# A two-layer encoder on one Trainium2 core: the first projection by k tile, products ahead of the data, earlier bias tables, a shorter sub-norm

## The chip, the cores and the metric

One core of a Trainium2 chip runs the whole kernel as one program. The metric is the device time of an execution in microseconds (us); lower is better. Engines are named as in the profile: PE is the matrix engine (PEld its weight loads), DVE the vector engine, ACT the scalar engine, POOL the GpSimd engine, SP the engine that issues nearly all DMAs here.

## What is computed

The input x is 512 tokens by 1024 channels in float32. Two layers follow one another, and each is a mixer with a residual sum and then an MLP with a residual sum:

- RMS norm, then layer 0's mixer: dilated sliding-window attention, 16 heads of 64 channels in three groups (6, 5 and 5 heads), with a bias from a 32 x 16 table, looked up by relative position, added to the logits; the groups' outputs are weighted by a softmax over their log-sum-exp.
- Layer 1's mixer: differential attention, 8 heads, two softmaxes per head, `a = p0 - lambda * p1` with lambda computed from a 4 x 64 input, `o = a @ v`, an RMS norm of o over its 128 channels (the sub-norm), then the output projection.
- Each MLP: `relu(x @ w_in)^2 @ w_out` with 4096 hidden channels.
- A last RMS norm.

The result has to agree with a float32 reference.

## The kernel before

**Layout and products.** Activations are kept transposed, eight tiles of 128 channels by 512 tokens (`hT[d]`). Every large float32 product is made of three products of rounded operands (`mm3`, L168 to L171): weights high by activations high, weights low times activations high, and the remaining cross term, each a 128x128 by 128x512 matmul. So each operand is split into a high part (an ACT copy, `whi`, `Ah`) and a low part (a DVE subtraction, `wlo`, `Al`). Weights come in units of 1 MB, 1024 rows by 256 columns for a projection. `fetch` (L140) reads a unit into `raw` and splits it in two halves by columns (L158 ACT, L159 DVE); `raw`, `whi` and `wlo` have two buffers each. `linear_steps` (L173) runs a unit: for each of its two tiles of 128 output columns eight k tiles of three products into one PSUM bank. There are eight banks: two `acc`, three `s`, two `t`, one `o`.

**The start.** L317 fetches the first unit (queries 0 to 255) in four pieces, with the reads of x between them. `Norm.feed` (L228) makes `Ah` on ACT and `Al` on DVE for each k tile and gathers the sum of squares, with POOL doing some squares and all sums (L236 to L243). L428 and L429 run the first queries and the first keys, column tile by column tile, into banks from `wide`; the results are held until the norm's factor is known (`rstd`, `rows`, then `release`), because the projection runs on the unnormalised x. `tables()` (L357) then looks up the bias tables: it reads the 33 x 2048 one-hot matrix, rounds it on ACT, makes eight 33-row products into `s` banks, copies them out on DVE (L375) and writes them to DRAM as `fd` (L376). `hankel` (L419) reads the biases of each query row back from `fd`, in rows that overlap: `B0` (six heads, 256 wide) and two parts of `B1` (L435 to L438).

**Layer 0's attention.** `probs0(p)` (L462) takes a pair of heads: logits on PE (L345, L346) into `s` banks, bias and row minimum in one DVE operation (L451), the exponential on ACT (L453), transposes on PE (L485) and a DVE copy (L487). The order in the program is probs0(0), probs0(1), qk0(1) (queries and keys of pair 2 and 3), values0(0), probs0(2), and so on (L569 to L592).

**Layer 1's attention.** `attend1` (L762) goes through 8 heads by 4 blocks of 128 queries: logits, softmaxes, `cf`, the combination on DVE (L785), transposes (L791), the product with v (L800) into one `o` bank for the four blocks of a head, the sub-norm of the block (`subnorm`, L802 to L812: a Square on ACT with its row sum, then five small POOL operations), after the fourth block one DVE product (`on`, L845) and the transposes back (`turn`, L814, L817). The head's `o` bank is free for the next head only when `on` has read it. `wo1_first` (L870) is the half of the output projection that needs heads 0 to 3 only, eight column tiles of 12 products each; `wo1_last` (L874) is the other half, five of whose column tiles are placed behind marked instructions by `tc.issue_after`.

**What sets the order.** A planner reorders the instructions by a simulated timeline: an instruction that comes later in the program may be placed ahead on its engine if its operands are ready and nothing earlier is. On the chip every engine then runs its own list strictly in that order. `tc.issue_after(x)` forbids the planner to put the block's PE instructions ahead of x. SP issues the DMAs in order, and a DMA that waits holds up those behind it.

Of the kernel before, what the change touches and what calls it, by code (L numbers as in the profile page):

```python
# [19 lines left out]
P = 128  # L20
# [7 lines left out]
MASKED = 1.0e30  # L28

# [52 lines left out]
def tile_encoder(ctx: ExitStack, tc: tile.TileContext, x, rel_bias, gains, norm_final_g,  # L82
# [18 lines left out]
    def s_tile():  # L101
        return ps_s.tile([P, 512], F32, tag="s", name="s_ps")
# [22 lines left out]

    hT = [hpool.tile([P, SEQ], F32, tag=f"h{d}", name=f"h{d}") for d in range(KT)]
# [13 lines left out]
    def fetch(between=None):  # L140
# [4 lines left out]
        src = w[r0:r0 + kt * P, c0:c0 + ncol].rearrange("(k p) c -> p k c", p=P)  # L145
# [8 lines left out]
        for i, (k, c) in enumerate(pieces):  # L154
            if between:
                nc.sync.dma_start(raw[:, k, c], src[:, k, c])
                between(i)
            nc.scalar.copy(hi[:, k, c], raw[:, k, c])  # L158
            nc.vector.tensor_sub(lo[:, k, c], raw[:, k, c], f32(hi[:, k, c]))  # L159
        ready.append((hi, lo))  # L160
# [59 lines left out]
    class Norm:  # L220
# [7 lines left out]
        def feed(self, d, start=False):  # L228
# [5 lines left out]
            if start:  # L234
                if d == 0:
                    nc.gpsimd.tensor_mul(self.acc, hT[d], hT[d])  # L236
                    return
                sq = spool.tile([P, SEQ], F32, tag="nsq", name="nsq")
                if d < 4:
                    nc.gpsimd.tensor_mul(sq, hT[d], hT[d])  # L240
                else:
                    nc.scalar.activation(sq, hT[d], AF.Square)
                nc.gpsimd.tensor_add(self.acc, self.acc, sq)  # L243
            elif d == 0:
                nc.scalar.activation(self.acc, hT[d], AF.Square)
            else:
                sq = spool.tile([P, SEQ], F32, tag="nsq", name="nsq")
                nc.scalar.activation(sq, hT[d], AF.Square)  # L248
                eng = nc.vector if d == KT - 1 else nc.gpsimd
# [61 lines left out]
    def load_x(*ds):  # L311
        for d in ds:
            nc.sync.dma_start(hT[d], x[d * P:(d + 1) * P, :])
# [29 lines left out]
    def logits(S, q, k, m, qs, ks):  # L343

        nc.tensor.matmul(S, q[m][:, qs], k[m][:, ks], start=True, stop=False)  # L345
        nc.tensor.matmul(S, q[2 + m][:, qs], k[m][:, ks], start=False, stop=True)  # L346
# [10 lines left out]
    def tables():  # L357
        tab = stp.tile([33, 16], F32, name="tab")
        nc.vector.memset(tab[32:33, :], MASKED)
        nc.sync.dma_start(tab[0:32, :], rel_bias)  # L360
        oh = stp.tile([33, E_END], F32, name="oh")
        nc.sync.dma_start(oh, onehot)
        ohr = stp.tile([33, E_END], F32R, name="ohr")
        nc.scalar.copy(ohr, oh)
        th = stp.tile([33, 16], F32R, name="th")
        tl = stp.tile([33, 16], F32R, name="tl")
        nc.vector.tensor_copy(th, tab)
        nc.vector.tensor_sub(tl, tab, f32(th))
        fsb = stp.tile([16, E_END], F32, name="fsb")
        for c in range(E_END // 512):  # L370
            s = slice(c * 512, (c + 1) * 512)
            ps = s_tile()
            nc.tensor.matmul(ps[0:16, :], th, ohr[:, s], start=True, stop=False)
            nc.tensor.matmul(ps[0:16, :], tl, ohr[:, s], start=False, stop=True)
            nc.vector.tensor_copy(fsb[:, s], ps[0:16, :])  # L375
        nc.sync.dma_start(fd, fsb)  # L376

        lam4 = stp.tile([P, 4, 64], F32, name="lam4")
        nc.sync.dma_start(lam4.rearrange("p a b -> p (a b)"),
                          b_lambda.rearrange("a b -> (a b)").unsqueeze(0).broadcast_to([P, 256]))  # L380
        lprod = stp.tile([P, 2, 64], F32, name="lprod")
        lsum = stp.tile([P, 2], F32, name="lsum")
# [24 lines left out]
    held = []  # L407

    def release():
        for f, ct, ps in held:  # L410
            f(ct, ps)

# [22 lines left out]
    hankel(B0, 0, 6, E_G0 + 64, 256)  # L435
    B1 = l0p.tile([P, 10, P], F32, name="B1", bufs=1)
    hankel(B1[:, 0:5, :], 6, 5, E_G1, P)
    hankel(B1[:, 5:10, :], 11, 5, E_G2, P)  # L438
# [130 lines left out]
    probs0(0)  # L569
    probs0(1)  # L570
    qk0(1)
    values0(0)
    probs0(2)
# [188 lines left out]
    def attend1(fill):  # L762
# [39 lines left out]
        def subnorm(b, r0, O, rs4):  # L802
# [144 lines left out]
```

## Time and profile before

| what | value |
|---|---|
| time, median of 3 runs | 1233.21 us (1232.64 to 1233.25) |
| profiled execution, its own time | 1232.82 us |
| profiled execution, span from first to last instruction | 1231.0 us |
| PE busy | 1206.0 us, 98% of the span, 6096 matmuls |
| DVE, ACT, POOL busy | 637.5, 499.3, 116.3 us |
| granted PE clock, mean | 0.993 |

The span is what the trace covers; the device time is 1.8 us longer. A PE row of the profile names the line, the output and input tiles and the shapes; "xN" is how many instructions were merged. The matmuls overlap in the trace, so the time from one start to the next is what counts, not the length shown. A float32 product that isn't split appears as two entries. Times in brackets are idle time of that engine before the instruction and what ended it.

### The profile page before, as it was taken

Reading aid. Unit: us, or ns where it says so; the run is one execution under the profiler, and the core shown is the slowest. Engines: PE = TensorE matmul, PEld = TensorE weight load, DVE = VectorE, ACT = ScalarE, POOL = GpSimd, SP = SyncE. Lnnn points to the kernel's source line nnn. Section 1 sums busy time; section 2 is a strip of 40 time slices with the busy share of each in tenths; the row PEclk is TensorE's granted clock in tenths of the full one; section 3 lists DMA queues with packets and bytes.
Section 4 is the critical chain, followed back from the end, with each engine's and each line's share of the span. In section 5 each row is a group of like instructions: output and inputs, shape, how many; then the busy total and the mean of one; then the engine's idle time right before and its main releaser. Section 6 shows DMA issues by size and latency. Waiting matters only on the chain.

```text
span 1231.0 us, 15250 instructions
## 1 busy us (share of the span) xinstructions
PE 1206.0 (98%) x6096; PEld 1020.2 (83%) x6096; DVE 637.5 (52%) x1039; ACT 499.3 (41%) x905; POOL 116.3 (9%) x219
## 2 busy tenths in 40 slices
PE   7989999999999999999999999998999999999997
PEld 5778878888888888888888998986888888888897
DVE  7764455645433434434478677673754334344333
ACT  5452433434322323313357667653544223133133
POOL 5000000210000000000201232322300000000012
PEclk9989999999999999999999999998999999999999
DMA  7261222233223333223422333121333223332211
GB/s 226 72 123 56 69 69 69 69 103 103 87 86 102 103 103 102 82 90 103 147 81 87 99 124 104 65 85 52 103 103 102 78 95 103 103 103 99 80 62 69
DMA packets 108307, 115.73 MB, mean 94 GB/s; under 512 B 4507, under 2 KB 101915, under 8 KB 108187
## 3 DMA queue, kind: packets, MB, share of 16 engines
q1 hardware_dynamic: 108236, 114.75, 30.0%
q8 instruction: 48, 0.79, 0.3%
q14 instruction: 23, 0.19, 0.0%
HBM read 112.50 MB, written 2.24 MB: 93 GB/s over the span
## 4 chain that ended last, share of the span: by engine, by line
PE 94%; DVE 2%; DMA 2%; ACT 1%; POOL 0%; issue 0%; SPq 0%; POOLq 0%; DVEq 0%; ACTq 0%
PE acc L169 15%; PE acc L171 15%; PE acc L170 15%; PE s_ps L170 13%; PE s_ps L171 13%; PE s_ps L169 13%; PE o_ps L800 2%; PE s_ps L345 1%; PE s_ps L346 1%; PE t_ps L791 1%; DMA B<-fd 1%; PE o_ps L525 1%; PE s_ps L494 1%; PE o_ps L529 1%; PE t_ps L485 0%; DMA h<-in_x_dram 0%
## 5 line engine op out<-in xcount | busy, mean ns | idle before, releaser
L158 ACT CAST whi<-raw 128x1024 fp32r<-128x1024 f32 (+1 forms) x194 | 192.7, 1039 | 392.8 <-PE s_ps L170 217.1
L159 DVE TENSOR_TENSOR wlo<-raw,whi 128x1024 fp32r<-128x1024 f32 (+1 forms) x194 | 233.7, 1241 | 22.9 <-ACT whi L158 22.5
L171 PE MATMUL acc<-Ah,wlo 128*128 128x512 f32 x472 | 185.9, 394 | 0.0
L169 PE MATMUL acc<-Ah,whi 128*128 128x512 f32 x472 | 185.8, 394 | 0.0
L170 PE MATMUL acc<-Al,whi 128*128 128x512 f32 x472 | 185.7, 393 | 0.0
L169 PE MATMUL s_ps<-Ah,whi 128*128 128x512 f32 x360 | 141.6, 394 | 5.7 <-ACT whi L158 5.5
L170 PE MATMUL s_ps<-Al,whi 128*128 128x512 f32 x360 | 142.1, 395 | 1.8 <-DVE Al L233 1.7
L171 PE MATMUL s_ps<-Ah,wlo 128*128 128x512 f32 x360 | 141.3, 393 | 0.0
L169 PEld LDWEIGHTS acc<-Ah,whi 128*128 128x128 f32 x472 | 89.0, 189 | 18.6 <-ACT sp L338 0.5
L171 PEld LDWEIGHTS acc<-Ah,wlo 128*128 128x128 f32 x472 | 88.8, 188 | 18.7 <-DVE wlo L159 0.5
L170 PEld LDWEIGHTS acc<-Al,whi 128*128 128x128 f32 x472 | 88.9, 188 | 18.1 <-issue 0.5
L169 PEld LDWEIGHTS s_ps<-Ah,whi 128*128 128x128 f32 x360 | 68.2, 190 | 20.3 <-ACT whi L158 5.5
L170 PEld LDWEIGHTS s_ps<-Al,whi 128*128 128x128 f32 x360 | 68.1, 189 | 17.6 <-DVE Al L233 3.8
L171 PEld LDWEIGHTS s_ps<-Ah,wlo 128*128 128x128 f32 x360 | 68.3, 190 | 14.2 <-DVE wlo L159 0.3
L644 ACT ACTIVATE u<-u 128x512 f32<-128x512 f32 x64 | 40.0, 628 | 96.6 <-DVE u L643 95.9
L250 POOL TENSOR_TENSOR nacc<-nacc,nsq 128x512 f32<-128x512 f32 x18 | 27.5, 1529 | 527.1 <-ACT nsq L248 526.6
L653 DVE TENSOR_TENSOR h<-h,s_ps 128x512 f32<-128x512 f32 x33 | 22.7, 688 | 105.4 <-PE s_ps L171 105.4
L643 DVE SCALAR_TENSOR_TENSOR u<-s_ps,rB 128x512 f32<-128x512 f32 x40 | 27.6, 691 | 83.8 <-PE s_ps L171 77.1
L775 DVE CUSTOM_DVE_ANT_0 p<-s_ps,bias 128x512 f32<-128x512 f32 x64 | 43.4, 688 | 31.0 <-PE s_ps L346 20.8
L171 PE MATMUL s_ps<-Bh,wlo 128*128 128x512 f32 x152 | 59.2, 389 | 0.0
L169 PE MATMUL s_ps<-Bh,whi 128*128 128x512 f32 x152 | 59.2, 389 | 0.0
L170 PE MATMUL s_ps<-Bl,whi 128*128 128x512 f32 x152 | 59.1, 389 | 0.0
(237 smaller groups left out, 2269.0 us busy)
## 6 DMA issues: line engine op xcount, KB each, us to landing
raw<-in_mlp_w_in_dram SPq DMA_DIRECT2D x32, 1024.0 KB, 5.3
raw<-in_mlp_w_out_dram SPq DMA_DIRECT2D x32, 1024.0 KB, 5.2
raw<-in_b_w_qkv_dram SPq DMA_DIRECT2D x12, 1024.0 KB, 5.2
raw<-in_a_w_qkv_dram SPq DMA_DIRECT2D x11, 1024.0 KB, 5.2
bias<-fd SPq DMA_DIRECT2D x16, 448.0 KB, 3.6
raw<-in_a_w_o_dram SPq DMA_DIRECT2D x4, 1024.0 KB, 5.2
raw<-in_b_w_o_dram SPq DMA_DIRECT2D x4, 1024.0 KB, 5.2
h<-in_x_dram SPq DMA_DIRECT2D x8, 256.0 KB, 5.1
```

Of the source, the lines that this page charges most:

```text
L158: nc.scalar.copy(hi[:, k, c], raw[:, k, c])
L159: nc.vector.tensor_sub(lo[:, k, c], raw[:, k, c], f32(hi[:, k, c]))
L169: nc.tensor.matmul(ps, ahi, bhi, start=first, stop=False)
L170: nc.tensor.matmul(ps, ahi, blo, start=False, stop=False)
L171: nc.tensor.matmul(ps, alo, bhi, start=False, stop=last)
L250: eng.tensor_add(self.acc, self.acc, sq)
L345: nc.tensor.matmul(S, q[m][:, qs], k[m][:, ks], start=True, stop=False)
L643: nc.vector.scalar_tensor_tensor(u, ps, 0.0, nm.rB, op0=ALU.max, op1=ALU.mult)
L644: nc.scalar.activation(u, u, AF.Square)
L653: nc.vector.tensor_add(hT[ct], hT[ct], ps)
L775: nc.vector.tensor_tensor_reduce(out=xt, in0=S, in1=bias[h][m][:, b * P:b * P + SEQ], scale=1.0, scalar=3.0e38, op0=ALU.add, op1=ALU.min, ...
L800: marks["PV"] = nc.tensor.matmul(O[:, b, :], aT[:, k, :], v[:, k, es], start=k == 0, stop=k == NB - 1)
```

## The change

- **First units by k tile.** `fetch` loses its special form. The first two units (first queries, first keys) are read in slices of one k tile: for each d, x's tile (256 KB) and 128 KB of each unit, 24 reads in all. `split_first(d)` makes the operands of k tile d; then four banks (three `s`, one `acc`) each get three products of that k tile. All squares are now made by ACT, and POOL only adds (the last sum is DVE's).
- **Idle products.** `WARM` = 14 float32 products of the identity with itself stand ahead of everything on PE, into a `t` bank.
- **Tables.** The one-hot matrix is read by a DMA that POOL issues, straight into the rounded type. The four parts of the table are made after k tiles 2 to 5, in `t` banks, and copied out by ACT. `B0` is read next; the two `B1` reads come after the second unit of keys; lambda's operations come after values0(0).
- **Second queries.** `rstd` and `rows` get a high priority. The second unit of queries follows at once, into the `o` bank and an `acc` bank, and is held; the four first banks are released after its first product. Its two tiles are taken out after probs0(0) and probs0(1), and the second unit of keys runs after that.
- **Sub-norm.** The factor is folded: `es = EPS * s0^2` is made early on POOL, the Square carries 1/128, and behind it stand two POOL operations, a sum and a power.
- **Output projection.** Of `wo1_first`, the third and fourth column tile of the second unit may not stand ahead of the last logits of head 7's block 2 and block 3.

```diff
+WARM = 14
...
+    idle = t_tile()
+    for i in range(WARM):
+        nc.tensor.matmul(idle[:, 0:P], ident, ident, start=True, stop=True)
...
-        parts = 2 if w is b_w_qkv or w is b_w_o else 2
-        pieces = [(slice(0, kt), slice(c * ncol // parts, (c + 1) * ncol // parts)) for c in range(parts)]
-        if between:
-            pieces = [(slice(k, k + 4), c) for _, c in pieces for k in (0, 4)]
-        else:
-            nc.sync.dma_start(raw, src)
...
+        nc.sync.dma_start(raw, w[r0:r0 + kt * P, c0:c0 + ncol].rearrange("(k p) c -> p k c", p=P))
+        for i in range(2):
+            c = slice(i * ncol // 2, (i + 1) * ncol // 2)
+            nc.scalar.copy(hi[:, :, c], raw[:, :, c])
+            nc.vector.tensor_sub(lo[:, :, c], raw[:, :, c], f32(hi[:, :, c]))
...
-    load_x(0)
-    fetch(lambda i: load_x(*((1, 2), (3, 4), (5,), (6, 7))[i]))
-    for d in range(KT):
-        norm.feed(d, True)
...
+    def load_first(d):
+        nc.sync.dma_start(hT[d], x[d * P:(d + 1) * P, :])
+        for src, raw, hi, lo in first:
+            nc.sync.dma_start(raw[:, d, :], src[:, d, :])
+
+    def split_first(d):
         norm.feed(d, True)
+        for src, raw, hi, lo in first:
+            nc.scalar.copy(hi[:, d, :], raw[:, d, :])
+            nc.vector.tensor_sub(lo[:, d, :], raw[:, d, :], f32(hi[:, d, :]))
+        norm.square(d, True)
...
+    def load_tables():
+        nc.vector.memset(tab[32:33, :], MASKED)
+        nc.sync.dma_start(tab[0:32, :], rel_bias)
+        nc.gpsimd.dma_start(ohr, onehot)
+
+    def table(c):
+        if c == 0:
+            nc.vector.tensor_copy(th, tab)
+            nc.vector.tensor_sub(tl, tab, f32(th))
+        s = slice(c * 512, (c + 1) * 512)
+        ps = t_tile()
+        nc.tensor.matmul(ps[0:16, :], th, ohr[:, s], start=True, stop=False)
+        nc.tensor.matmul(ps[0:16, :], tl, ohr[:, s], start=False, stop=True)
+        nc.scalar.copy(fsb[:, s], ps[0:16, :])
+        if c == 3:
+            nc.sync.dma_start(fd, fsb)
...
-    run(linear_steps(0, KT, 256, norm.xs, out_q0, bank=wide, hold=held))
-    run(linear_steps(0, KT, 256, norm.xs, out_k0, bank=wide, hooks=[(4, norm.rstd), (8, lambda: norm.rows(-0.125)), (12, release)]))
-    tables()
+    load_first(0)
+    load_first(1)
+    load_tables()
+    for d in range(2, KT):
+        load_first(d)
+    banks = [s_tile(), s_tile(), s_tile(), acc_tile()]
+    for d in range(KT):
+        split_first(d)
+        for i, ps in enumerate(banks):
+            _, _, hi, lo = first[i // 2]
+            s = slice((i % 2) * P, (i % 2 + 1) * P)
+            mm3(ps, hi[:, d, s], lo[:, d, s], norm.xs[0][d], norm.xs[1][d], d == 0, d == KT - 1)
+        if 2 <= d < 6:
+            table(d - 2)
...
     hankel(B0, 0, 6, E_G0 + 64, 256)
+    held = []
+    with tc.high_priority():
+        norm.rstd()
+        norm.rows(-0.125)
+
+    def release():
+        for i, ps in enumerate(banks):
+            (out_q0, out_k0)[i // 2](i % 2, ps)
+
+    spare_banks = [acc_tile, o_tile]
+    run(linear_steps(2, KT, 256, norm.xs, out_q0, bank=lambda: spare_banks.pop()(),
+                     hooks=[(1, release)], hold=held))
...
     probs0(0)
+    for f, ct, ps in held[:1]:
+        f(ct, ps)
     probs0(1)
-    qk0(1)
+    for f, ct, ps in held[1:]:
+        f(ct, ps)
+    run(linear_steps(2, KT, 256, norm.xs, out_k0))
+    hankel(B1[:, 0:5, :], 6, 5, E_G1, P)
+    hankel(B1[:, 5:10, :], 11, 5, E_G2, P)
     values0(0)
+    lam()
...
+            es = l1p.tile([P, 1], F32, tag="es", name="es", bufs=4)
+            nc.gpsimd.tensor_scalar(es, st[:, b, 2:3], st[:, b, 2:3], EPS, op0=ALU.mult, op1=ALU.mult)
+            return pr[0], es
...
-            nc.scalar.activation(sq, O[:, b, :], AF.Square, accum_out=ss)
-            rs = rs4[:, b, :]
-            nc.gpsimd.tensor_mul(rs, ss, r0)
-            nc.gpsimd.tensor_mul(rs, rs, r0)
-            nc.gpsimd.tensor_scalar(rs, rs, 1.0 / P, EPS, op0=ALU.mult, op1=ALU.add)
-            nc.gpsimd.tensor_tensor(rs, rs, mhalf[:, 0:1], op=ALU.pow)
-            nc.gpsimd.tensor_mul(rs, rs, r0)
+            nc.scalar.activation(sq, O[:, b, :], AF.Square, scale=1.0 / math.sqrt(P), accum_out=ss)
+            nc.gpsimd.tensor_add(ss, ss, es)
+            nc.gpsimd.tensor_tensor(rs4[:, b, :], ss, mhalf[:, 0:1], op=ALU.pow)
...
+        after = {(1, 2): ("S", 7, 2), (1, 3): ("S", 7, 3)}
         for c in range(2):
-            yield from linear_steps(4 * c, 4, 512, ([OH1[k] for k in range(4)], [OL1[k] for k in range(4)]), add_h)
+            hi, lo = next_w()
+            for t in range(4):
+                mark = marks[after[c, t]].ins if (c, t) in after else None
+                with tc.issue_after(mark) if mark else nullcontext():
...
```

## Rows read from the trace of the kernel before

**Rows 1.** The page's first part: busy time, share of the span and instructions of each engine.
```profile
PE 1206.0 (98%) x6096; PEld 1020.2 (83%) x6096; DVE 637.5 (52%) x1039; ACT 499.3 (41%) x905; POOL 116.3 (9%) x219
```

**Rows 2.** The waits of PE over the whole span: who waited for whom, us in total, times, longest.
```profile
PE s_ps L169 <- ACT whi L158: 5.5, 1, 5.5
PE t_ps L817 <- DVE on L845: 5.2, 1, 5.2
PE s_ps L345 <- DVE mnN L451: 4.7, 1, 4.7
```

**Rows 3.** Stretches of the span: its bounds and length, then busy us and instructions of PE, PEld, DVE, ACT and POOL, the granted PE clock, the DMA share and GB/s.
```profile
0.00:16.75 16.75, 9.26 (x18) 5.43 (x19) 11.21 (x13) 10.70 (x16) 11.66 (x14) 1.00 0.87 272
65.80:70.50 4.70, 0.00 (x0) 0.01 (x1) 0.84 (x5) 0.44 (x2) 0.00 (x0) 0.73 0.97 105
70.50:74.86 4.36, 4.34 (x20) 4.30 (x21) 3.97 (x11) 4.35 (x14) 0.00 (x0) 0.51 0.94 123
831.61:844.91 13.30, 7.60 (x40) 7.22 (x41) 6.65 (x12) 4.79 (x15) 5.58 (x14) 0.74 0.25 79
300.00:400.00 100.00, 100.00 (x443) 82.82 (x442) 42.05 (x49) 32.12 (x42) 0.00 (x0) 1.00 0.29 95
```

**Rows 4.** The timeline of the first 17 us: start, length, engine, line, operation, tiles, count, and in brackets the idle time before it.
```profile
0.99 0.29 POOL masks.py:199 TENSOR_SCALAR_AFFINE_SELECT ident<-ident 128x128 f32<-128x128 f32 x1
...
1.17 0.42 SPq L313 DMA_DIRECT2D h<-in_x_dram  x1
...
4.14 0.72 ACT L232 ACTIVATE Ah<-h,gT 128x512 fp32r<-128x512 f32 x1 [1.93 <-DMA h<-in_x_dram]
...
4.86 0.62 ACT L158 CAST whi<-raw 128x512 fp32r<-128x512 f32 x1
4.90 0.81 DVE L233 SCALAR_TENSOR_TENSOR Al<-h,gT,Ah 128x512 fp32r<-128x512 f32 x1 [2.37 <-ACT Ah L232]
...
5.63 0.68 DVE L159 TENSOR_TENSOR wlo<-raw,whi 128x512 fp32r<-128x512 f32 x1
...
9.02 3.40 POOL L243 TENSOR_TENSOR nacc<-nacc,nsq 128x512 f32<-128x512 f32 x2
...
9.53 1.77 DVE L159 TENSOR_TENSOR wlo<-raw,whi 128x512 fp32r<-128x512 f32 x1
...
13.03 0.80 PE L170 MATMUL s_ps<-Al,whi 128*128 128x512 f32 x1 [1.72 <-DVE Al L233]
...
16.75 0.40 PE L169 MATMUL acc<-Ah,whi 128*128 128x512 f32 x1
```

**Rows 5.** Two stretches of the first 50 us, columns as in rows 3.
```profile
10.00:15.00 5.00, 3.28 (x8) 2.09 (x8) 5.00 (x4) 3.94 (x7) 4.84 (x4) 1.00 1.10 354
40.00:50.00 10.00, 10.00 (x43) 6.99 (x42) 9.74 (x16) 8.38 (x13) 0.00 (x0) 1.00 0.33 105
```

**Rows 6.** DMA issues over the whole span: tiles, queue, count, KB each, median us from issue to landing.
```profile
raw<-in_a_w_qkv_dram SPq DMA_DIRECT2D x11, 1024.0 KB, 5.2
B<-fd SPq DMA_DIRECT2D x1, 768.0 KB, 11.3
B<-fd SPq DMA_DIRECT2D x2, 320.0 KB, 22.7
fd<-fsb SPq DMA_DIRECT2D x1, 128.0 KB, 2.5
```

**Rows 7.** The reads into `raw` in the first 90 us: us from issue to landing.
```profile
DMA to landing us min/median/max: 3.2/5.4/23.2
```

**Rows 8.** DVE's operations by line and shape in the stretch 40 to 60 us: count, then busy us, mean ns of one, and idle time before them.
```profile
L331 DVE TENSOR_TENSOR sp<-q,sp 64x512 fp32r<-64x512 f32 x6 | 4.1, 682 | 0.1
...
L159 DVE TENSOR_TENSOR wlo<-raw,whi 128x1024 fp32r<-128x1024 f32 x2 | 2.4, 1220 | 0.0
```

**Rows 9.** The same of DVE in the stretch 69.6 to 100 us.
```profile
L487 DVE COPY ptn<-t_ps 128x512 f32<-128x512 f32 x8 | 5.2, 685 | 1.0 <-PE t_ps L485 1.0
...
L451 DVE CUSTOM_DVE_ANT_0 xt<-s_ps,B 128x192 f32<-128x192 f32 x12 | 4.1, 352 | 8.7 <-DMA B<-fd 8.7
```

**Rows 10.** The timeline at the end of layer 1's attention, from the product of head 6's last block but one to the last block of head 7.
```profile
824.58 1.06 PE L800 MATMUL o_ps<-v,aT 128*128 128x128 f32 x8
825.39 0.47 PE L345 MATMUL s_ps<-k,qh 128*128 128x512 f32 x1
...
829.86 1.06 PE L800 MATMUL o_ps<-v,aT 128*128 128x128 f32 x8
...
830.98 0.39 PE L346 MATMUL s_ps<-k,ql 128*128 128x512 f32 x1
...
832.39 0.19 POOL L808 TENSOR_TENSOR rs<-ss,rr 128x1 f32<-128x1 f32 x1 [4.44 <-ACT sq L806]
...
835.96 0.69 DVE L845 TENSOR_TENSOR on<-o_ps,rs 128x512 f32<-128x512 f32 x1 [0.98 <-POOL rs L812]
...
836.80 1.08 PE L817 MATMUL t_ps<-ident,on 128*128 128x128 f32 x4 [5.19 <-DVE on L845]
...
843.56 1.16 PE L800 MATMUL o_ps<-v,aT 128*128 128x128 f32 x8 [0.52 <-ACT sq L806]
...
848.67 0.19 POOL L808 TENSOR_TENSOR rs<-ss,rr 128x1 f32<-128x1 f32 x1 [1.78 <-ACT sq L806]
...
850.34 0.69 DVE L845 TENSOR_TENSOR on<-o_ps,rs 128x512 f32<-128x512 f32 x1 [7.07 <-POOL rs L812]
```

More of the change, by code (lines that the diff above doesn't have):

```diff
@@ L1 @@
 import math
-from contextlib import ExitStack
+from contextlib import ExitStack, nullcontext
 import numpy as np
@@ L138, in unit, with fetch @@
         units.append((w, r0, kt, c0, nc_))
-    def fetch(between=None):
+    def fetch():
         if not units:
@@ L234, in feed, with square @@
             if start:
[L235 to L244, printed above, removed]
+                return
+            self.square(d, d == KT - 1)
+        def square(self, d, on_dve):
+            if d == 0:
                 nc.scalar.activation(self.acc, hT[d], AF.Square)
@@ L309, in tile_encoder @@
     nc.sync.dma_start(gT, gains)
-    def load_x(*ds):
-        for d in ds:
-            nc.sync.dma_start(hT[d], x[d * P:(d + 1) * P, :])
     norm = Norm(G_MIX0, "A")
-    load_x(0)
-    fetch(lambda i: load_x(*((1, 2), (3, 4), (5,), (6, 7))[i]))
-    for d in range(KT):
+    first = []
+    for _ in range(2):
+        w, r0, kt, c0, ncol = units.pop(0)
+        first.append((w[r0:r0 + kt * P, c0:c0 + ncol].rearrange("(k p) c -> p k c", p=P),
+                      *(wpool.tile([P, kt, ncol], dt, tag=t, name=t)
+                        for t, dt in (("raw", F32), ("whi", F32R), ("wlo", F32R)))))
+    def load_first(d):
[3 more added lines that the diff above has]
+    def split_first(d):
         norm.feed(d, True)
+        for src, raw, hi, lo in first:
+            nc.scalar.copy(hi[:, d, :], raw[:, d, :])
+            nc.vector.tensor_sub(lo[:, d, :], raw[:, d, :], f32(hi[:, d, :]))
+        norm.square(d, True)
     qT, kT = {}, {}
@@ L355, in tile_encoder, with lam @@
     nlam = const.tile([P, 1], F32, name="nlam")
-    def tables():
-        tab = stp.tile([33, 16], F32, name="tab")
+    tab = stp.tile([33, 16], F32, name="tab")
+    ohr = stp.tile([33, E_END], F32R, name="ohr")
+    th = stp.tile([33, 16], F32R, name="th")
+    tl = stp.tile([33, 16], F32R, name="tl")
+    fsb = stp.tile([16, E_END], F32, name="fsb")
+    def load_tables():
         nc.vector.memset(tab[32:33, :], MASKED)
         nc.sync.dma_start(tab[0:32, :], rel_bias)
[L361 to L378, printed above, removed]
+        nc.gpsimd.dma_start(ohr, onehot)
[10 more added lines that the diff above has]
+            nc.sync.dma_start(fd, fsb)
+    def lam():
+        lam4 = spool.tile([P, 4, 64], F32, tag="nsq", name="lam4")
         nc.sync.dma_start(lam4.rearrange("p a b -> p (a b)"),
                           b_lambda.rearrange("a b -> (a b)").unsqueeze(0).broadcast_to([P, 256]))
-        lprod = stp.tile([P, 2, 64], F32, name="lprod")
-        lsum = stp.tile([P, 2], F32, name="lsum")
+        lprod = spool.tile([P, 2, 64], F32, tag="nsq", name="lprod")
+        lsum = const.tile([P, 2], F32, name="lsum")
         nc.vector.tensor_mul(lprod, lam4[:, 0::2, :], lam4[:, 1::2, :])
@@ L870, in wo1_first @@
     def wo1_first():
+        after = {(1, 2): ("S", 7, 2), (1, 3): ("S", 7, 3)}
         for c in range(2):
[L872 removed]
+            hi, lo = next_w()
+            for t in range(4):
+                mark = marks[after[c, t]].ins if (c, t) in after else None
+                with tc.issue_after(mark) if mark else nullcontext():
+                    ps = acc_tile()
+                    s = slice(t * P, (t + 1) * P)
+                    for k in range(4):
+                        mm3(ps, hi[:, k, s], lo[:, k, s], OH1[k], OL1[k], k == 0, k == 3)
+                add_h(4 * c + t, ps)
     def wo1_last(on):
@@ L905, in tile_encoder @@
     woven(attend1(fill), fill, 1.5)
-    run(wo1_first())
+    wo1_first()
     nm = Norm(G_MLP1, "A")
```

28 lines of the change are left out of this document (7 added, 21 removed).

## The prediction, made before the change was run

> **What bounds the kernel now.** I read the page's busy times first: PE is busy for 98% of the span and DVE for 52% [rows 1], so a change pays only where PE stands or runs at its lower clock. PE's waits come next: three single waits of about 5 us are nearly all of them, and they lie in three places [rows 2]: before the first product, at the first softmax, where DVE waits 8.7 for `B0` [rows 9], and at a `turn` late in layer 1's attention. Then I cut the span there [rows 3]. In a quiet stretch 443 products take 100 us, 0.226 us each at the granted clock of 1.00, the 2.4 GHz level. Against that price:
>
> - Start: 18 products in the first 16.75 us are worth 4.1, so **12.7 us** are lost. 5.5 of it is the wait for data; the rest is stalls and the lower level: from 13.03 to 16.75 eight products start, one each 0.465 [rows 4], about twice 0.226.
> - Middle: no product from 65.80 to 70.50, then 4.36 us at a granted clock of 0.51, which is 1.2 GHz [rows 3]. Those 20 entries are twelve logits of 256 columns (half of 0.226 each) and eight transposes of 128 columns (0.10, the step of L800 in rows 10: 0.81 for 8). They are worth 2.2, so **6.9 us** are lost.
> - Tail: 40 entries of 128 columns from 831.61 to 844.91 are worth 4.0, so **9.3 us** are lost.
>
> In all 28.9 us; the change reaches for each of the three.
>
> **The start, part by part.** *Idle products.* The identity is ready at 1.28 [rows 4]. An unsplit float32 product is two entries of 0.10 [rows 10], so 14 take 2.8 us at the upper level and 5.6 at the lower. PE starts low. What it did before its step halved: it worked 3.7 us without a gap from 13.03 to 16.75, 4.36 after the middle's wait, and 6.8 from 836.80 to 843.56, where eight entries of L800 take 1.16 again [rows 3, 4, 10]. If the idle products do it in 3.7, at 5.1, nine are done and five more take 1.0: the end is 6.1. If not in time: 1.4 + 5.6 = 7.0, and the real products start slow. The first real product could come at 5.3 at best (`Ah` and `whi` in rows 4). I take **6.6**, between the two.
>
> *Slabs.* A k tile brings 512 KB; the queue moved 354 GB/s at the start [rows 5], so 1.5 us a slab. SP issues three reads at 0.42 [rows 4], 1.3 us, plus the table's small read: all landed by about 17. PE needs 12 x 0.226 = 2.71 a slab, so reads are not the bound. ACT: `Ah` 0.72, two casts of 256 columns at about 0.41 (from 0.62 for 512 and 1.04 for 1024), a Square about 0.6: 2.15, and 0.6 more where it copies a table part; just within PE's pace with the table's products (2.71 + 2 x 0.23). DVE: 0.81 + 2 x 0.41 = 1.63 alone; but while POOL adds, a DVE operation of 0.68 takes 1.77 and an add 1.70 [rows 4]. In 1.70 us DVE does 0.65 us of its work, so a slab takes 1.70 + 0.98 = **2.68**: level with PE, no reserve. If all of DVE's work went at the slow rate it would be 4.2 a slab and DVE the bound (12 us worse over eight); if POOL cost nothing, 1.63. One add per slab is nearest to 2.68. I allow 1.0 us of PE waits.
>
> *The POOL-issued read.* No read in the trace is issued by POOL. Nearest rows: the 128 KB write took 2.5 us, `B0` 11.3 [rows 6]. Issued near 5, it lands between 7.5 and 16.5; the first table product stands in PE's list after the third slab, at 6.6 + 3 x 2.71 = 14.7. I take none, as the size is nearer to the first; bound 2 us. POOL worked 4.84 of 5 us beside a DVE busy 5.00 of 5 [rows 5], so it isn't shut out. The Trainium skill (SBUF — State Buffer, "SBUF: two separate sides") warns of the opposite: POOL cannot write a DMA's descriptors while DVE holds the port pair they share. Taken for every DVE operation, the read would wait for DVE's first pause; that is a rival below, at 1235 instead of 1219.9.
>
> *Hand-over.* First queries and keys now end together: 6.6 + 1.0 + 21.7 + 8 table products (1.8) = **31.1**. Both `whi` buffers are in use nearly to the end; the queries' one is free six products earlier, at 29.7. The third unit's first cast (1.04, `whi` halves) ends near 30.8, its `wlo` (1.22, rows 8) near 32.1; two products can run before it, so PE lacks 0.6, and `rstd`/`rows` fill part. Its read takes 5.2 [rows 6] and can start when DVE ends the eighth slab, near 25: 30. I allow **1.2** in all. The loss becomes 6.6 + 1.0 + 1.2 = 8.8: gain **3.9**.
>
> **The middle.** The table is written after the sixth slab: 6.6 + 1.0 + 16.3 + 1.8 = 25.7, copy 0.6, write 2.5, `B0` read 11.3: there at about **40**, not at 70. The first softmax can't come much earlier: from 31.1 DVE has four scalings, the third unit's `wlo` (2.4) and most of twelve half-tile subtractions at 0.68 [rows 8]: about 42. So the wait goes. What is late next is DVE itself, 97% busy in 40 to 50 [rows 5]. Its list from 31.1 until two pairs of heads are through: 10.9 + three units 7.3 + second queries 4.5 + 16 softmaxes at about 0.47 with their read of the minimum + 8 copies at 0.69 [rows 8, 9] = 35.7 us. PE's list there: second queries, second keys and first values at 48 x 0.226 = 10.8 each, two pairs (32 logits at 0.113, 32 transposes at 0.10) 6.8, the norm's 16 small entries 1.6: 40.8. So PE still bounds, if fed in time. `B1` behind the keys delays weight reads that queue behind it (up to 22.7, rows 6), but those are needed after 53. I keep a third of the loss, 2.4 us, since DVE has little reserve and the copies already waited 1.0 for their transposes [rows 9]: gain **4.5**, bounds 0 and 6.9, and below nothing by the rivals. At no cost: ACT loses the one-hot's rounding and DVE the table copies, and lambda's operations move to where nothing waits for them before layer 1.
>
> **The tail.** Sub-norm: five POOL operations took 1.67 us from the first to `on` where DVE left them alone, and 3.57 where it worked beside them [rows 10]. Two operations are worth about 1.0 and 2.0. `es`, `reciprocal` and the rest are off the path. From head 6's last product (829.86) to the `turn` PE had only one pair of logits and a last product to do. Now 12 products (2.7 us) stand behind the last logits, and 12 behind block 2's. From the end of that product at 830.7 to a `turn`: Square, two POOL operations and `on`, about 1.7 + 2.0 + 0.9 = 4.6 crowded, 3.6 not, against 0.5 + 2.7 of PE work. So 0.4 to 1.4 us stay of 5.2, and PE no longer drops to the lower level. Left over: 0.9 there; three waits of 0.5 of a block's product for the Square of the block before (843.56 in rows 10); up to 2.0 where the 24 products stood before, at 821 to 831. 0.9 + 1.5 + 2.0 = 4.4: gain **4.9**, bounds 0 and 7.8.
>
> **The sum.** 3.9 + 4.5 + 4.9 = 13.3 us. The profiled execution took 1232.82 (span 1231.0 and 1.8 around it), so 1219.5. The median of the runs stands 0.4 above it: **1219.9**. At best 12.7 - 7.3 = 5.4, 6.9 and 7.8 make 1213.
>
> **Rivals.**
> - *DVE starves PE in the middle.* The second column tile of the keys (5.4) and the first values (10.8) need banks that DVE frees only after the second pair, if the planner keeps program order. PE's list without them ends at 31.1 + 40.8 - 16.2 = 55.7, DVE's at 66.8: 11 us idle and 2.1 at the lower level, instead of 2.4. Time 1230.6. For: DVE's 97% [rows 5]. Against: the planner fills idle DVE time with what is ready. 0.12.
> - *The tail doesn't pay*: the moved products leave an equal hole before, or the `turn` keeps waiting because DVE's `wlo` (1.22) sits ahead of `on`. 1224.8. For: the old place kept PE busy up to 831. Against: the waits there were for DVE and POOL [rows 2], which a later product covers. 0.11.
> - *Slower: third weights behind `B0`.* If SP's list has that read after `B0`'s, it isn't issued before the table has landed at 28.8 and queues behind 11.3 us: a read behind the `B` reads took 23.2 to land, the median is 5.4 [rows 7]. It lands near 45, PE stands from 31.1 + 1.6 to 46.3, some 13.6 us, and some 4 more at the lower level: 17.6 instead of 1.2 makes 1236. It decides if the `raw` buffer frees later than 28.8; I get 25. 0.06.
> - *The POOL read is held up*: DVE has no pause before slab eight, so the read lands near 27.5 and PE stands 12.8 us from 14.7, with 2 at the lower level: 1235. This is the rule above as a mechanism of this kernel; against it stands POOL's 4.84 of 5 us. 0.02.
> - *The idle products don't do what they should*: they end at 7.0 with the clock still low, and the first 3.7 us and more of real work run at half rate: 1.9 + 0.4 worse, 1222. 0.05.
>
> **How the numbers follow.** About 0.2% (2.5 us: below 1230.7 or above 1235.7) is what a measurement of this kernel can tell from no change. The forecast has 0.64. The first rival counts half as faster and half as no change, the second and the fifth as faster, the fourth as no change. Faster: 0.64 + 0.06 + 0.11 + 0.05 = 0.86; same: 0.06 + 0.02 = 0.08; slower: 0.06. The range goes from 1212 to 1231: all three places at their best, up to the middle starved.
>
> **What the changed profile would show.** Steps of 0.23 from the first real product on, before 8 us; `s_ps` and `acc` products without a gap of over 1 us to about 31; `B<-fd` issued near 29 and no DVE wait for it; no PE wait of over 2 us at `turn`, granted clock 1.00 at 830 to 845. Wrong would be: a wait of PE on the third unit's `whi`, a hole of over 5 us at 45 to 70, or the old 13 us at the tail.

## The result and the profile after

The changed kernel took **1221.24 us** in the median of four runs (1220.31 to 1222.06); the kernel before, timed beside it, 1233.23. The ratio is 0.9902, 95% interval 0.9885 to 0.9919: 12.0 us faster. The profiled execution took 1220.61, its span is 1218.4 (before: 1231.0).

The page's busy times, against [rows 1]: POOL falls from 116 to 88 us, PE hardly moves.
```profile
PE 1203.0 (99%) x6124; PEld 1020.3 (84%) x6124; DVE 628.9 (52%) x1052; ACT 500.6 (41%) x922; POOL 87.5 (7%) x145
```
PE's waits over the span, against [rows 2], longest first: ahead of the first product stands now the idle products' wait for the identity, the `turn` is gone, and the wait at the first softmax (L474, before L451) is still there, 3.6 us instead of 4.7.
```profile
PE s_ps L349 <- DVE mnN L474: 3.6, 1, 3.6
PE t_ps L130 <- POOL ident masks.py:199: 2.5, 1, 2.5
PE o_ps L833 <- ACT aT L826: 2.1, 2, 1.4
PE o_ps L552 <- ACT vn L540: 0.3, 1, 0.3
```
Four stretches of the changed kernel, columns as in [rows 3]: the idle products, the work from the first real product to the next hole, the hole at the first softmax, what is left of the hole at the tail.
```profile
2.48:7.96 5.48, 5.48 (x28) 5.48 (x29) 1.67 (x4) 2.57 (x5) 0.00 (x0) 1.00 0.98 288
7.96:57.90 49.94, 49.94 (x230) 39.07 (x228) 32.50 (x58) 26.36 (x51) 1.42 (x5) 1.00 0.73 170
57.90:65.74 7.84, 4.25 (x21) 3.82 (x21) 7.07 (x19) 6.21 (x18) 0.00 (x0) 0.78 0.51 169
826.50:832.05 5.55, 3.47 (x30) 3.00 (x28) 4.15 (x7) 3.60 (x11) 3.05 (x5) 1.00 0.28 80
```
PE has no gap for 50 us from its first real product. Then 21 entries take 7.84 us, 3.6 of it empty; the mean granted clock of the stretch is 0.78, and the trace's record has it at 0.5, the level of 1.2 GHz, for 3.4 us from 62.0 on.

To set all runs side by side I summed PE's loss by stage: for each product, the time to the next one's start less the usual step (lower quartile) of its line and shape; the start counts from zero and leaves the idle products out. Microseconds, from the profiled executions:
```
                        start  middle  80 to  240 to  640 to  tail    end
                        to 50  50-80   240    640     810     810-860
before                  13.4    7.4    10.6   1.0     4.8     10.8    1.3
changed                  9.3    6.0     9.9   1.5     5.0      4.0    1.7
sub-norm + hold only    13.2    7.1    10.4   1.0     4.7      4.2    1.3
hold only               13.8    7.4    10.6   0.9     4.8      4.3    1.2
sub-norm only           13.6    7.5    10.7   1.5     4.8      8.6    1.7
head only                8.3    7.4     9.6   0.4     4.8      9.8    0.8
no idle products        10.7    7.7     9.8   0.4     4.7      4.0    0.8
sums on POOL             9.8    8.3    10.0   1.0     4.9      3.9    1.2
identity first           8.9    6.3     9.7   0.9     4.9      3.9    1.2
B1 behind 6th read       9.1    1.2     9.2   1.1     5.0      3.7    1.2
B1 behind 5th read       9.3    1.2     9.2   1.1     5.0      3.7    1.2
  + long sub-norm        8.3    1.3     8.8   0.5     5.0      3.6    0.9
  + 10 idle products     8.3    1.3     8.8   0.5     5.0      3.5    0.9
  + identity first       7.5    1.4     9.1   1.7     5.1      3.7    1.6
```
("+" rows build on "B1 behind 6th read"; the last has 10 idle products as well.) So the change gained 4.1 us at the start, 1.4 in the middle and 6.8 at the tail, where 3.9, 4.5 and 4.9 were forecast. Each row is one execution. The 1.4 is the least certain: the same order in the middle lost 7.4 with the head only and 7.7 without idle products, where PE waited 4.0 and 4.4 us and the clock stood at 0.5 for 6.8 us instead of 3.4. By those two rows the middle gained nothing.

**The start**, against [rows 4], timeline columns as there:
```profile
1.25 0.76 POOL L370 DMA_DIRECT2D ohr<-in_onehot_dram  x1 [0.32 <-issue]
...
2.11 0.32 POOL masks.py:199 TENSOR_SCALAR_AFFINE_SELECT ident<-ident 128x128 f32<-128x128 f32 x1
2.48 5.72 PE L130 MATMUL t_ps<-ident 128*128 128x128 f32 x28 [2.48 <-POOL ident masks.py:199]
...
6.38 0.71 ACT L321 CAST whi<-raw 128x256 fp32r<-128x256 f32 x2 [1.18 <-DMA raw<-in_a_w_qkv_dram]
...
7.96 0.48 PE L167 MATMUL s_ps<-Ah,whi 128*128 128x512 f32 x1
...
8.28 0.40 PE L168 MATMUL s_ps<-Al,whi 128*128 128x512 f32 x1
```
POOL issues the one-hot's read, 0.76 us, ahead of the operation that makes the identity, which comes at 2.11 instead of 0.99. The idle products fill PE to 7.96, the first data were cast at about 6.8, and the first real steps are 0.31 and 0.23, so at the upper level, 2.4 GHz.

**The middle**, a timeline of SP, ACT, DVE and PE:
```profile
28.14 0.33 SPq L382 DMA_DIRECT2D fd<-fsb  x1
30.77 3.16 SPq L425 DMA_DIRECT2D B<-fd  x3
36.07 25.21 SPq L153 DMA_DIRECT2D raw<-in_a_w_qkv_dram  x3
...
57.45 1.99 ACT L156 CAST whi<-raw 128x1024 fp32r<-128x1024 f32 x2 [10.21 <-DMA raw<-in_a_w_qkv_dram]
...
58.53 2.36 DVE L157 TENSOR_TENSOR wlo<-raw,whi 128x1024 fp32r<-128x1024 f32 x2 [6.91 <-ACT whi L156]
60.81 0.35 DVE L474 CUSTOM_DVE_ANT_0 xt<-s_ps,B 128x192 f32<-128x192 f32 x1
...
61.66 0.36 PE L349 MATMUL s_ps<-sp,sp 128*128 128x256 f32 x1 [3.59 <-DVE mnN L474]
```
Read it from below. PE waits for the first softmax (60.81), which waited for nothing of its own: `B0` was read at 30.77 and landed 12.0 later, its first logits started at 47.6. It stands behind `wlo` of the fifth weight unit in DVE's list; DVE stood 6.91 us for the cast, and ACT had stood 10.21, from 47.24, for the raw read. That read was issued at 36.07, right behind **all three** `B` reads ("x3" at 30.77), and took 21.3 to land. The `B1` reads are written behind the second keys in the program, but the planner placed them right behind `B0`'s, ahead of the fifth raw read.

**The tail**, against [rows 10]:
```profile
823.18 0.19 POOL L840 TENSOR_TENSOR ss<-ss,es 128x1 f32<-128x1 f32 x1
...
823.45 0.55 POOL L841 TENSOR_TENSOR rs<-ss,mhalf 128x1 f32<-128x1 f32 x1
...
824.11 0.68 DVE L874 TENSOR_TENSOR on<-o_ps,rs 128x512 f32<-128x512 f32 x1
...
825.10 0.60 PE L846 MATMUL t_ps<-ident,on 128*128 128x128 f32 x4
...
828.43 1.16 PE L833 MATMUL o_ps<-v,aT 128*128 128x128 f32 x8 [1.40 <-ACT aT L826]
...
830.70 1.16 PE L833 MATMUL o_ps<-v,aT 128*128 128x128 f32 x8 [0.68 <-ACT aT L826]
```
From the first POOL operation to `on` 0.93 us instead of 1.67 to 3.57, a `turn` without a wait, and behind it two waits of another kind, 2.1 in all.

### The profile page after: what moved, and what is told of

Its sections match the earlier page's. It is cut to its first block, busy times and chain, and to the rows that moved or that the text cites. A ratio compares the mean times of both kernels' runs of the same rounds, so it can differ in the third digit from the quotient of the medians.

```text
span 1218.4 us, 15236 instructions
## 1 busy us (share of the span) xinstructions
PE 1203.0 (99%) x6124; PEld 1020.3 (84%) x6124; DVE 628.9 (52%) x1052; ACT 500.6 (41%) x922; POOL 87.5 (7%) x145
## 4 chain that ended last, share of the span: by engine, by line
PE 95%; DMA 2%; DVE 1%; ACT 1%; issue 0%; POOL 0%; POOLq 0%; ACTq 0%; DVEq 0%
PE acc L167 15%; PE acc L169 15%; PE acc L168 15%; PE s_ps L167 13%; PE s_ps L168 13%; PE s_ps L169 13%; PE o_ps L833 2%; DMA raw<-in_a_w_qkv_dram 2%; PE s_ps L349 1%; PE s_ps L350 1%; PE t_ps L824 1%; PE o_ps L548 1%; PE s_ps L517 1%; PE o_ps L552 1%; PE t_ps L508 1%; PE t_ps L130 0%
## 5 line engine op out<-in xcount | busy, mean ns | idle before, releaser
L156 ACT CAST whi<-raw 128x1024 fp32r<-128x1024 f32 x188 | 188.3, 1049 | 399.1 <-PE s_ps L168 201.6
L157 DVE TENSOR_TENSOR wlo<-raw,whi 128x1024 fp32r<-128x1024 f32 x188 | 224.3, 1231 | 28.4 <-ACT whi L156 27.7
L167 PE MATMUL s_ps<-Ah,whi 128*128 128x512 f32 x352 | 137.4, 391 | 0.0
L168 PE MATMUL s_ps<-Al,whi 128*128 128x512 f32 x352 | 137.2, 390 | 0.0
L169 PE MATMUL s_ps<-Ah,wlo 128*128 128x512 f32 x352 | 136.9, 390 | 0.0
L808 ACT ACTIVATE p<-p,st 128x512 f32<-128x512 f32 x64 | 46.2, 723 | 27.8 <-DVE st L805 27.0
```

The source lines that it names most:

```text
L156: nc.scalar.copy(hi[:, :, c], raw[:, :, c])
L157: nc.vector.tensor_sub(lo[:, :, c], raw[:, :, c], f32(hi[:, :, c]))
L167: nc.tensor.matmul(ps, ahi, bhi, start=first, stop=False)
L168: nc.tensor.matmul(ps, ahi, blo, start=False, stop=False)
L169: nc.tensor.matmul(ps, alo, bhi, start=False, stop=last)
L808: nc.scalar.activation(pt, xt, AF.Exp, bias=mn, scale=-1.0, accum_out=st[:, b, 2 + m:3 + m])
```

## The experiments

Each timed run stands beside runs of the kernel before on its own chip (median 1232.7, 1233.0 and 1233.1 in the three groups), so ratios are the thing to compare.

**1. Which part carries what** (four kernels, one group).

*Both tail parts alone*, put into the kernel before:
```
+ after = {(1, 2): ("S", 7, 2), (1, 3): ("S", 7, 3)}   # held products, and
...
+ nc.gpsimd.tensor_add(ss, ss, es)                     # the short sub-norm
+ nc.gpsimd.tensor_tensor(rs4[:, b, :], ss, mhalf[:, 0:1], op=ALU.pow)
```


> The kernel before with both tail parts (sub-norm in two POOL operations, 24 output products held back) and nothing else of the change. Theory (the parts add up; by the PE loss of the two traces 10.1 us at 825 to 850 became 3.4): 6.7 us faster than before, 1226.5, with the tail rows of the changed kernel. The forecast's own size was 4.9: 1228.3. Rival (the tail gains only together with the head, or the head carries the result): under 2 us, above 1231.

Measured: 1226.23, ratio 0.9948 (0.9936 to 0.9960), 6.5 us faster, near the 6.7 expected.

*The head alone*: the changed kernel with these lines undone.

> The changed kernel with the sub-norm and the place of the 24 output products as before: only start, tables and order of the head. Theory: start worth 3.9 and middle 1.4, so 1227.9, and the wait of about 5 us at the turn is back. The forecast's sizes (3.9 + 4.5) would give 1224.8. Rival (the two ends don't add, something later than 60 us gives part of it back): above 1229.5.

Measured: 1226.44, ratio 0.9951 (0.9939 to 0.9963), 6.3 us, and a wait of 5.2 at the `turn`. It lies between the two sizes. In the profiled execution the idle products ended at 7.06 instead of 7.96 (below), and the start lost 8.3 instead of 9.3; the middle lost as much as before. 6.5 and 6.3 make 12.8, the change as a whole 12.0: tail and head add up within a microsecond.

*The short sub-norm alone*, without the hold:

> The kernel before with the short sub-norm alone; the 24 products stand where they stood. Theory: three POOL operations less on the chain from a block's last product to its turn, 1.0 to 2.0 us at the last block and a little at the three before: the wait at the turn falls from about 5 to 3 to 4 us, 1230.5 to 1231.5. Rival (the sub-norm is the whole of the tail's gain): 1226.5.

Measured: 1230.30, ratio 0.9983 (0.9974 to 0.9991), 2.4 us. PE's waits and the timeline there:
```profile
PE t_ps L816 <- DVE on L844: 4.2, 1, 4.2
```
```profile
832.23 0.19 POOL L810 TENSOR_TENSOR ss<-ss,es 128x1 f32<-128x1 f32 x1 [2.33 <-ACT sq L809]
832.45 2.35 DVE L159 TENSOR_TENSOR wlo<-raw,whi 128x1024 fp32r<-128x1024 f32 x2
832.50 1.58 POOL L811 TENSOR_TENSOR rs<-ss,mhalf 128x1 f32<-128x1 f32 x1
...
834.79 0.67 DVE L844 TENSOR_TENSOR on<-o_ps,rs 128x512 f32<-128x512 f32 x1
```
From the first POOL operation to `on` 2.56 us, 1.0 less than the 3.57 of [rows 10], and the wait is 1.0 shorter; the tail as a whole loses 8.6 instead of 10.8. POOL is done at 834.08, but `on` starts only at 834.79, when the `wlo` ahead of it in DVE's list has ended (832.45 + 2.35 = 834.80). With this order in DVE's list a chain shorter still would leave the wait where it is. In the kernel before, the same `wlo` ran beside the five POOL operations:
```profile
832.63 2.35 DVE L159 TENSOR_TENSOR wlo<-raw,whi 128x1024 fp32r<-128x1024 f32 x2
```

*The hold alone*, with five POOL operations:

> The kernel before with the 24 output products held behind the logits of head 7's blocks 2 and 3, sub-norm as before (five POOL operations). Theory: 12 products (2.7 us) stand under each of the last two chains and keep the clock up, 4 to 6 us faster: 1227.5 to 1229; 1 to 2 us of wait at the turn stay, since the chain is the long one. Rival (an equal hole opens where the products stood): within 1.5 us of before.

Measured: 1225.55, ratio 0.9945 (0.9933 to 0.9956), 7.1 us: **all of the tail's gain**, and more than expected. In its timeline the five POOL operations are still there (the first is shown), 1.67 to `on`, and the `turn` waits for nothing:
```profile
828.74 0.19 POOL L808 TENSOR_TENSOR rs<-ss,rr 128x1 f32<-128x1 f32 x1 [2.56 <-ACT sq L806]
...
830.41 0.69 DVE L845 TENSOR_TENSOR on<-o_ps,rs 128x512 f32<-128x512 f32 x1 [0.43 <-POOL rs L812]
...
831.66 0.60 PE L817 MATMUL t_ps<-ident,on 128*128 128x128 f32 x4
...
832.73 1.22 DVE L159 TENSOR_TENSOR wlo<-raw,whi 128x1024 fp32r<-128x1024 f32 x1
...
834.99 1.16 PE L800 MATMUL o_ps<-v,aT 128*128 128x128 f32 x8 [1.40 <-ACT aT L793]
```
`on` ends at 831.10, and the `turn` starts at 831.66, when the held products have run: the chain is covered, with 0.56 to spare. The hold did a second thing: the next `wlo`, which stood ahead of `on`, now comes behind it, at 832.73, since the cast into its `whi` buffer (ACT, 831.63) has to wait for held products; and the five operations took 1.67, not 3.57. Work under the chain and a `wlo` out of its way were not tried apart. By an estimate from these rows, at 3.57 `on` would have ended near 833.0, and the `turn` would have waited 1.3. The two later waits, 2.1 in all, are the same with either sub-norm; what makes them was not tried.

**2. The hole in the middle.** *B1's reads behind the fifth and sixth raw reads*:
```
- hankel(B1[:, 0:5, :], 6, 5, E_G1, P)
- hankel(B1[:, 5:10, :], 11, 5, E_G2, P)
  values0(0)
+ with tc.issue_after(marks["raw"].ins):     # the latest raw read, the sixth unit's
+     hankel(B1[:, 0:5, :], 6, 5, E_G1, P)
+     hankel(B1[:, 5:10, :], 11, 5, E_G2, P)
```


> The changed kernel with the two reads of B1 issued behind the raw reads of the fifth and the sixth unit, instead of right behind B0's. Theory (the raw read queued behind B1's holds ACT, ACT holds DVE, DVE holds the first softmax): the fifth raw read lands near 45 to 50 instead of 57.4, the wait of 3.6 us at the first softmax's transposes goes to under 1 and the clock stays up: 4 to 5 us faster than the changed kernel, 1216 to 1217. Rival (DVE's list alone makes the first softmax late): the first softmax still starts near 60, 1220 to 1221. Second rival (B1 now is late): PE waits for the near heads' next softmaxes, 1221 or more.

Measured: **1215.20**, ratio 0.9853 (0.9838 to 0.9868), 6.0 us below the changed kernel, more than the 4 to 5 expected. Its timeline, and two stretches over the place of the hole:
```profile
30.59 0.37 SPq L426 DMA_DIRECT2D B<-fd  x1
35.89 2.64 SPq L154 DMA_DIRECT2D raw<-in_a_w_qkv_dram  x2
38.58 6.76 SPq L426 DMA_DIRECT2D B<-fd  x2
...
47.08 2.00 ACT L157 CAST whi<-raw 128x1024 fp32r<-128x1024 f32 x2
...
53.57 0.34 DVE L475 CUSTOM_DVE_ANT_0 xt<-s_ps,B 128x192 f32<-128x192 f32 x1
```
```profile
50.00:58.00 8.00, 8.00 (x42) 6.81 (x42) 7.85 (x20) 4.27 (x14) 0.00 (x0) 1.00 0.57 142
58.00:66.00 8.00, 8.00 (x53) 7.20 (x52) 7.74 (x17) 6.22 (x16) 0.00 (x0) 1.00 0.20 64
```
The fifth raw read, issued at the same moment, is there when ACT comes to it at 47.08, with no wait; the first softmax starts 7.2 us earlier; PE has no gap and the clock stays at 1.00. DVE is 98% busy from 50 to 58 and still doesn't bound PE. `B1` landed later and nothing waited for it.

*Behind the fifth only*, ahead of the sixth:

> The changed kernel with B1's two reads behind the fifth unit's raw read only, ahead of the sixth's. Theory (it is the fifth read, the one that ACT and DVE stand behind, that matters): first softmax near 50, no wait of over 1 us there: 1215 to 1216, or up to 2 more if the sixth read, now behind B1, is late for the values. Rival (the sixth read behind B1 holds ACT and DVE just as the fifth did, some units later): a new wait of 3 us or more between 55 and 75, 1219 to 1221.

Measured: 1215.60, ratio 0.9858 (0.9845 to 0.9872); PE has no new wait. The sixth read, now behind `B1`, took 19.9 us to land and ACT stood 1.5 us for it, which PE didn't feel. It is the fifth read that mattered.

**3. The start.** *Without the idle products*:
```
- for i in range(WARM):
-     nc.tensor.matmul(idle[:, 0:P], ident, ident, start=True, stop=True)
```


> The changed kernel without the 14 idle products. Theory (they raise the clock, 1.00 when the first real product comes): the first real product comes at 6.4 to 8.0, but 0.45 apart for some 4 us, about 2 us slower than the changed kernel, 1223. Rival (the reads set the start, not the products): first product at 6.4, half-rate time hidden under the wait for slabs, 1220 to 1221.5.

Measured: 1223.00, ratio 0.9917 (0.9904 to 0.9931), as the theory had it. The interval overlaps with the changed kernel's, so the size isn't settled; the trace shows the mechanism, and the start's loss grows by 1.4. PE's timeline:
```profile
7.07 1.22 PE L164 MATMUL s_ps<-Ah,whi 128*128 128x512 f32 x2 [7.07 <-ACT whi L318]
...
9.37 0.63 PE L165 MATMUL s_ps<-Al,whi 128*128 128x512 f32 x1
9.80 0.63 PE L164 MATMUL acc<-Ah,whi 128*128 128x512 f32 x1
...
15.07 0.40 PE L164 MATMUL acc<-Ah,whi 128*128 128x512 f32 x1
15.31 0.39 PE L165 MATMUL acc<-Al,whi 128*128 128x512 f32 x1
```
The first product comes 0.9 earlier, but the steps are 0.43, the level of 1.2 GHz, until 11.9.

*Six of the sums on POOL*, as the text before the result took them to be:
```
- norm.square(d, True)
+ norm.square(d, d == KT - 1)
```


> The changed kernel with six of the sums of squares in the start on POOL instead of DVE, as the forecast took them to be. Forecast's price: a DVE slab grows from 2.15 (idle POOL) to 2.68 us, level with PE's 2.71: 0 to 1 us slower, 1221 to 1222. Rival (all of DVE's work goes at the slow rate beside POOL): 4.2 a slab, DVE bounds the start, 8 to 12 us slower, 1229 to 1233. Other rival (the adds cost DVE nothing): 1221.

Measured: 1223.62, ratio 0.9922 (0.9910 to 0.9934), 2.4 us above the changed kernel, though the intervals overlap a little: none of the prices named. DVE by shape from 10 to 20 us, and SP:
```profile
L322 DVE TENSOR_TENSOR wlo<-raw,whi 128x256 fp32r<-128x256 f32 x7 | 5.9, 881 | 0.0
L231 DVE SCALAR_TENSOR_TENSOR Al<-h,gT,Ah 128x512 fp32r<-128x512 f32 x3 | 4.3, 1434 | 0.0
```
```profile
24.20 1.01 SPq L153 DMA_DIRECT2D raw<-in_a_w_qkv_dram  x2
...
32.65 3.05 SPq L425 DMA_DIRECT2D B<-fd  x3
```
In the changed kernel these two operations take 0.41 and 0.73. Four slabs, from 8.52 to 20.43, took 3.0 each, or 2.7 without the 1.27 that the table's `tl` took among them (0.16 in the changed kernel); the forecast was 2.68. PE bears it: the start's loss grows by 0.5 only, and 0.3 of that is that the idle products ended later. But the third and fourth raw reads leave at 24.20 instead of 21.16, so `fd`'s write runs beside them and takes 3.9 instead of 2.6, the `B` reads leave 1.9 later, and the fifth raw read behind them lands at 59.6: the middle loses 2.3 more. Not all of that is the sums': the same middle without them lost 6.3 to 7.7 in three other runs, and without idle products the fifth read landed as late. The Trainium skill (SBUF — State Buffer, "SBUF: two separate sides") calls the port pair that DVE and POOL share an exclusive lock, against DVE operations with two SBUF inputs too. The trace agrees in kind: both operations have two SBUF inputs, and take about twice as long in the mean.

*The one-hot's read behind the identity*:
```
+ with tc.issue_after(made):          # made: the identity's last instruction
      nc.gpsimd.dma_start(ohr, onehot)
```


> The changed kernel with POOL's read of the one-hot issued behind the making of the identity. Theory: the identity is there near 1.4 instead of 2.5, the 28 idle entries end near 6.8 instead of 7.96, the first real product comes at 6.8 to 7.1: about 1 us faster, 1220. Rival (the slabs' reads set the pace, not the identity): the time saved at the first product is lost at the second or third slab: 1221.

Measured: 1220.65, ratio 0.9902 (0.9889 to 0.9916): no change. The first real product comes at 7.28 instead of 7.96, but the third slab of x is late (ACT stands 1.33 us for it at 10.10), and of 0.7 us 0.4 stays at the start and none in the time.

**4. On top of the mended middle** (one group, all with B1's reads behind the raw reads). *The long sub-norm*, five operations as before:

> The changed kernel with B1's reads behind the fifth and sixth raw reads (1215.2 us), but with the sub-norm of before, five POOL operations. Theory (the held products cover the chain whether it is short or long; the hold alone and the hold with the short sub-norm took the same time, 1225.55 and 1226.23): 1214.5 to 1215.5, and no wait at the turn. Rival (the short sub-norm is worth its 1.0 to 2.0 us once the middle no longer hides it): 1216.2 or more.

Measured: 1214.51, ratio 0.9849 (0.9835 to 0.9862), within the noise of the run with the short one (1215.20). With the hold in place these runs show no gain from the short sub-norm.

*Ten idle products* (`WARM = 10`):

> The changed kernel with B1's reads behind the fifth and sixth raw reads (1215.2 us), and 10 idle products instead of 14. Theory (the idle products stand in front of the first real one by some 0.9 us, and the first slab's cast is ready near 6.8): 20 entries end near 6.7 to 6.9, the first real product comes at 6.8 to 7.1; the steps may be 0.43 for up to a microsecond: 1214.5 to 1215.2. Rival (with less idle work the clock rises later by as much as is saved): first products at 0.43 for 2 us or more, 1215.2 to 1216.5.

Measured: 1214.12, ratio 0.9846 (0.9832 to 0.9859). That is a little below the range expected. The first product comes at 6.58 at the upper level. The group's two kernels with 14 took 0.4 us (long sub-norm) and 1.5 us (behind the fifth only) more, which the intervals don't separate.

*Ten, and the identity first*:

> As the run with 10 idle products, and with POOL's read of the one-hot behind the making of the identity. Theory (slab reads set the start once the idle products are out of the way): idle entries end near 5.7, first real product at 6.4 to 6.8, steps of 0.43 until about 7 to 8, then waits for slabs: 1214.5 to 1215.5. Rival (the earlier work raises the clock earlier, and every slab is in time): 1213.5 to 1214.5.

Measured: **1213.14** (1213.03 to 1213.78), ratio 0.9840 (0.9826 to 0.9853), the fastest kernel here, 8.1 us below the changed one and below both times expected. PE's timeline:
```profile
1.35 4.43 PE L131 MATMUL t_ps<-ident 128*128 128x128 f32 x20 [1.35 <-POOL ident masks.py:199]
5.64 0.74 PE L169 MATMUL s_ps<-Ah,whi 128*128 128x512 f32 x2
```
The first real product starts 2.3 us earlier than in the changed kernel. Against ten idle products alone it is 1.0 us faster; its slowest run (1213.78) is ahead of the fastest there (1213.92), but the intervals of the ratios overlap. Why the identity's order seems worth something here and nothing in part 3 has not been taken apart: here it comes with fewer idle products and without the hole of the middle behind it.

## Why the prediction came out near, and where it was wrong

1219.9 against 1221.24, in the range and on the right side; but two of the three terms were mis-sized, and the errors (start +0.2, middle -3.1, tail +1.9) partly cancel. The start's own closeness is in part luck: the first product came 1.4 late, the waits took 0.8 less than allowed, and the loss before is 13.4 by the table instead of 12.7.

- **Idle products: right in kind, late by 1.4.** The first real product came at 7.96, not 6.6. The text took the identity at 1.28 from the old trace and asked of POOL's new read only when it lands, not what it does to POOL's own list: its issue stands ahead of the identity. 28 entries of 0.21 from 2.48 on end near 8.4, somewhat earlier if the clock rises on the way; it did, before the first real product.
- **DVE's slab: wrong reading of the code, without harm.** `split_first` calls `square(d, True)`, so the sums are DVE's, not POOL's as the text and the section on the change say. DVE needs 0.73 + 2 x 0.41 + 0.67 = 2.2 a slab (1.9 from start to start), POOL has no sums to make, and nothing slows DVE. The price for what the text had in mind was 2.68 and measures 2.7 to 3.0. Slab waits and hand-over, 1.0 and 1.2 allowed, took 1.4 together. The third weights' read left at 21.16, so the rival that puts it behind `B0` fell in that place.
- **POOL's read: right.** Issued at 1.25 (the text had near 5), it landed in 4.9 us, between the ends of 2.5 and 11.3. DVE had little to do then, so the rule of a held-up read was not put to the test.
- **The middle: the failed step.** "`B1` behind the keys delays weight reads that queue behind it (...), but those are needed after 53." Neither half held: `B1` went right behind `B0`, and the read behind it was needed at 47.2. The wait for `B0` went, as forecast (it landed at 42.8, about 40 expected), and a raw read took its place, with a hole of 3.6 us, under the 5 that the text had named as its sign of being wrong: 1.4 of 4.5 gained, or nothing by the rows of head only and no idle products. The third rival had the mechanism (a read behind the `B` reads takes over 20 us) and looked at the third unit, two units too early. The price was in [rows 7] all along. Experiment 2 gives 4.8 us of loss back, so the middle was worth 6.2, not 4.5; and the rival in which DVE starves PE is refuted by a DVE at 98% and a PE without a gap.
- **The tail: right place, wrong part.** 4.9 forecast, 6.8 measured. The left-over was sized well (4.0 against 4.4); the loss before was undercounted, since it was taken from 831.6 to 844.9 and is 10.8 from 810 to 860. The text gave the shorter sub-norm a share in closing the wait; experiment 1 shows the hold doing it all. The rival with DVE's `wlo` ahead of `on` had seen what kept the wait at 4.2 under the short sub-norm alone; the hold also took that `wlo` out of the way, which the text didn't foresee. The feared equal hole where the products stood did not open: with the hold alone the loss from 640 to 810 is unchanged and that from 810 to 860 is 4.3.

## What to carry to other kernels

Program order is not queue order where a planner places the instructions: before pricing a DMA that moves, ask which reads stand behind it in its queue, and when the in-order engines behind those reads come to them. Where work that is ready could be held back under a long chain, shortening the chain as well bought nothing here; measure the two apart before keeping both. Before shortening a chain, look at what the engine at its end has to do first: here a 2.35 us `wlo` would have been the next limit. POOL paid 0.76 us in its own list to issue a DMA, and what had been first there, an identity of 0.3 us, came that much later.

## What was not expected of the hardware

The step of PE halves at quite different moments of the same idle list. With the first entry at 2.48 or 2.49 it fell from 0.21 toward 0.11 at 5.42 (head only), 5.59 (long sub-norm), 6.27 (ten idle products), 6.90 (B1 behind the sixth read), 7.34 (changed), 7.35 (B1 behind the fifth) and 7.98 (sums on POOL). With the first entry at 1.34 or 1.35 it fell at 5.35 in one execution (ten, identity first); in the other (identity first) it was still 0.21 at 6.84, and the first shorter step began at 7.05. So an earlier start is not sure to bring an earlier rise, and the first real product moves by up to 1.2 us (7.06 to 8.25) behind one and the same list of 28. These are single executions of different kernels; what sets the moment stays open.

The granted clock reads 1.00 in all these stretches, also where the steps are at the lower level. The trace's record of the clock begins only at the rise, at 7.40 in the changed kernel, 5.51 with the head only, 11.93 without idle products and 16.73 before, and the column counts the time ahead of it as 1.00. Ahead of the first rise, read the level from the steps.
